# A two-layer decoder trunk in split fp32r matmuls: sums of squares as two fp32r matmuls behind seven k, a gate block copied out of PSUM, input rows 320 floats apart

## The chip, the cores and the metric

One NeuronCore of a Trainium2 chip runs the whole program. The metric is the device time of one execution in microseconds (us); the figure of the kernel before is the median of three runs. One execution was also profiled; its own time and its span (first to last instruction) stand in the table below.

## The reference, cut to what matters

256 tokens of width 1024 go through two layers and a last RMSNorm, all in float32:

```python
hdn = modulate(rmsnorm(x, norm1_g[l]), shift1, scale1)
proj = hdn @ w_in[l]                       # latents, sb q/k/v, mb q/k/v, three gates
q  = rmsnorm(q_lat, q_norm_g[l]) @ w_uq[l]
kv = rmsnorm(c_kv, kv_norm_g[l]) @ w_ukv[l]
merged = g_a * (o_mla @ w_o_mla[l]) + g_b * (o_sb @ w_o_sb[l]) + g_c * (o_mb @ w_o_moba[l])
x = x + gate1[:, None, :] * (merged @ w_out[l])
hdn = modulate(rmsnorm(x, norm2_g[l]), shift2, scale2)
x = x + gate2[:, None, :] * (jnp.square(jax.nn.relu(hdn @ w_ff1[l])) @ w_ff2[l])
```

`rmsnorm` divides a token by the root of its mean square and multiplies by a gain; `modulate` multiplies by 1 + scale and adds a shift. shift, scale and gate come from a conditioning vector (`w_ada`). The gates g_a, g_b, g_c are sigmoids of columns of `proj`.

## The kernel before, in words

**Layout.** Activations lie transposed: the 1024 features are eight tiles (k = 0 to 7) of 128 partitions by 256 tokens. Every float32 product is made of three fp32r matmuls: weights and activations are each split into a high part (rounded to fp32r) and a low part (the rest), and high·high, high·low and low·high are added up in PSUM (`mm3`, L348 to L351, and L983 to L986 for the second MLP product). A sum of squares instead is a plain float32 matmul of a 256-column tile with a matrix of minus ones (`minus`), which adds over the partitions and leaves the sum in every partition (`Rms.sum`, L301).

**Jobs.** The work is a list of jobs. A job is 1 MB of weights fetched by one DMA of the SP queue into one of three buffers, split in four pieces (L184 on ACT for the high part, L185 on DVE for the low part), and used by two or more parts of 24 matmuls each. The parts of a job with `half` (L353) go over k from 0 to 7 inside one half of 128 output features. Splits of later jobs are spread over the parts of earlier ones. Attention and the two latent norms are side tasks, which are let in between parts (`pump`). Outside the stretches named next, a scheduler orders each engine's instructions by program position and readiness, with a cost model of its own; each engine then runs its list strictly in order.

**Buffers.** `mm` is a pool of three PSUM buffers (128 x 2 x 256), which all outputs of such parts take in turn; a new output waits until the reader of the buffer's last content is done. `slot` is a pool of eight large SBUF buffers; `t512` is a pool of four 128 x 2 x 256 ones.

**Seams.** Where a residual update ends and the next normed product begins, an order written by hand takes over (`seam` L869, `overlap` L926, under a manual schedule). There are three such seams: output projection to MLP in layer 0, MLP to the next layer, output projection to MLP in layer 1. A fourth, the tail, makes the last norm. In a seam:
- `ahead` (L815) has already scaled x by its gain without the root, as high and low rows `xh` and `xl` of 258 columns, which are 256 tokens and the shift vector twice. Both are whole slots with rows 258 floats apart, behind a phase of 48 floats.
- `pre_mm` (L366) multiplies these rows with the weights of the next two jobs, a and b (6 matmuls of 258 columns per k and job, 96 in all), since the root can be applied to the product afterwards.
- The sum of squares is made meanwhile: tiles 0 to 5 are added into `acc` on DVE, the squares of tiles 6 and 7 are kept apart (`late`). `sum(more=True)` issues the matmuls of `acc` and of tile 6, then come the last residual update (tile 7) and `pre_mm` of job a for k = 0, 1, 2, then the matmul of tile 7's squares, then k = 3 to 7.
- `root` (L310) is four ACT and three DVE instructions in a chain; two weight pieces of the job after b are split behind it; then `modulate` (L336) makes the finished activation, tile by tile, as a high part on ACT (L342) and a low part on DVE (L345). The job after b is the first that reads this activation, k by k.

**Latent norms.** `lat_norm` (L657) runs twice a layer (2 and 6 tiles) as a side task: squares, adds, `sum`, `root`, then scaled tiles in high and low parts.

**Gates and latent keys.** `gates(1)` makes four blocks of the stick-breaking gate. A block's `done` is `sigmoid` (L133): Abs of the PSUM block on ACT, Exp, Ln, one DVE instruction that reads the PSUM block again (L137), and Exp. Behind the fourth block comes the job of `wukv`: two PSUM blocks `kn` of latent keys, each copied out by four ACT instructions (L741), and two blocks `mvps` of values; then come the jobs of `wuq`.

Of the kernel before, what the change touches and what calls it, by code (L numbers as in the profile page):

```python
# [11 lines left out]
F32 = mybir.dt.float32  # L12
# [9 lines left out]
S = 256  # L22
# [18 lines left out]
def trunk(ctx, tc, xT, heads, pos, signs, masks, gfin, wada, win, wkpe, wuq, wukv, wo, wout, wff1, wff2, out):  # L41
# [7 lines left out]
    def mmps(name):  # L49
        return psum.tile([128, 2, 256], F32, name=name, tag="mm", bufs=3)  # L50
# [7 lines left out]
    def slot(name, dt=F32, shape=(128, 8, 256)):  # L58
        a, b = shape[1:]
        t = big.tile([128, PHASE + 8 * (S + 2)], dt, name=name, tag="slot", bufs=8)  # L60
        return t[:, PHASE:PHASE + a * b].rearrange("p (a b) -> p a b", b=b)

    def t512(name, dt=F32):
        return work.tile([128, 2, 256], dt, name=name, tag="t512", bufs=4)
# [68 lines left out]
    def sigmoid(dst, src, tmp):  # L133
        nc.scalar.activation(tmp, src, AF.Abs)
        nc.scalar.activation(tmp, tmp, AF.Exp, scale=-1.0)
        nc.scalar.activation(tmp, tmp, AF.Ln, bias=1.0)
        nc.vector.scalar_tensor_tensor(tmp, src, 0.0, tmp, op0=OP.min, op1=OP.subtract)  # L137
        nc.scalar.activation(dst, tmp, AF.Exp)
# [101 lines left out]
    def split(dh, dl, src):  # L240
        nc.scalar.activation(dh, src, AF.Copy)
        nc.vector.tensor_sub(dl, src, dh.bitcast(F32))  # L242
# [34 lines left out]
    class Rms:  # L277
# [15 lines left out]
                nc.vector.tensor_add(self.acc, self.acc, sq[:, 0, :])  # L293
            self.i += 1

        def square_late(self, a):
            sq = t256("sql")
            nc.scalar.activation(sq, a, AF.Square)
            self.late.append(sq)

        def sum(self, more=False):  # L301
            if self.ps is None:
                self.ps = mmps("ssum")[:, 0, :]
            terms = ([self.acc] if self.acc is not None else []) + self.late
            for t in terms:
                nc.tensor.matmul(self.ps, minus, t, start=self.first, stop=not more and t is terms[-1])
                self.first = False
            self.acc, self.late = None, []
# [57 lines left out]
    def pre_mm(jb, ps, xg, ks):  # L366
        for k in ks:
            for i in range(2):
                c = k * 256 + i * 128
                for n, (w, a) in enumerate(((jb.wh, xg[0]), (jb.wh, xg[1]), (jb.wl, xg[0]))):  # L370
                    nc.tensor.matmul(ps[:, i, 0:258], w[:, c:c + 128], a[:, k, :], start=k == 0 and n == 0,  # L371
                                     stop=k == KT - 1 and n == 2, skip_group_check=True)

    def job(src, f, kts, act, done, ncol=256, before=None, pre=None):
# [220 lines left out]
    def layer(l):  # L595
# [94 lines left out]
        def gate_done(b, u):  # L690
            def done(ps, j):
                if u == 0:
                    T["g", b] = slot("gate")
                g = T["g", b][:, 2 * u:2 * u + 2, :]
                sigmoid(g, ps, g)
            return done

# [117 lines left out]
        def ahead(k, sec):  # L815
            if sec == 5 and l + 1 == L:
                return
            l2, gofs, sc, sh = (l, 56, 4, 3) if sec == 2 else (l + 1, 48, 1, 0)
            if k == 0:
                rms["gs"] = gs = gain(l2, gofs, sc)  # L820
                rms["xs"] = xh, xl = tuple(slot(n, F32R, (128, KT, S + 2)) for n in ("xh", "xl"))
                m = mods[l2][:, sh * 8:sh * 8 + 8, None].to_broadcast([128, KT, 2])
                split(xh[:, :, S:], xl[:, :, S:], m)
            xh, xl = rms["xs"]
            g = rms["gs"][:, k:k + 1]
            nc.scalar.activation(xh[:, k, :S], x[:, k, :], AF.Copy, scale=g)
            nc.vector.scalar_tensor_tensor(xl[:, k, :S], x[:, k, :], g, xh[:, k, :S].bitcast(F32),
                                           op0=OP.mult, op1=OP.subtract)

        def x_done(u, ps, sec):  # L830
# [9 lines left out]
        def x_last(i, ps, sec):  # L840
            def go():
                x_one(6 + i, ps, sec)
                final(6 + i, sec)
                rms["q"].square_late(x[:, 6 + i, :])
                ahead(6 + i, sec)
            if i == 0:
                go()
            else:
                rms["last"], rms["end"] = go, ps
# [76 lines left out]
        def overlap(then, n):  # L926
            l2, sh = (l, 3) if then == 2 else (l + 1, 0)
            a, b = jobs[n:n + 2]
            split_to(n + 1, PIECES)
            pa, pb = atps("pre0"), atps("pre1")  # L930
            rms["q"].sum(more=True)
            rms["last"]()
            pre_mm(a, pa, rms["xs"], range(3))
            rms["q"].sum()
            pre_mm(a, pa, rms["xs"], range(3, KT))
            split_to(n + 2, PIECES // 2)
            r = rms["q"].root()
            split_to(n + 2, PIECES)
            pre_mm(b, pb, rms["xs"], range(KT))
            modulate(l2, r, rms["gs"], sh, range(KT))  # L940
            skip.update((n, n + 1))
            return lambda: [split_to(later(n, 3), 2), a.pre(pa, r), split_to(later(n, 3), 4), b.pre(pb, r)]
# [332 lines left out]
```

## Time and profile before

| | us |
|---|---|
| Median of three runs | 935.19 (934.09 to 935.22) |
| Profiled execution, its own time | 934.94 |
| Its span | 933.2 |
| PE busy (TensorE matmuls) | 916.7 (98%) |
| DVE busy (VectorE) | 731.0 (78%) |
| ACT busy (ScalarE) | 600.5 (64%) |
| Mean granted TensorE clock | 0.999 of full speed |

PE is the matmul engine, PEld its weight loads, which overlap it. A matmul's record is longer than the distance to the next one's start, because matmuls are pipelined: what a matmul costs in a stream is that distance. A plain float32 matmul leaves two records. In a timeline, neighbouring instructions of one kind are merged ("x2"), and a bracket tells how long the engine sat idle and what ended that. Idle time of an engine other than the bound costs nothing by itself.

### The profile page before, as it was taken

How to read it: one execution, taken by the hardware profiler on the slowest of the kernel's cores; microseconds unless marked ns; L12 is line 12 of the kernel's file. 1: busy time of each engine (PE TensorE's matmuls, PEld its weight loads, DVE VectorE, ACT ScalarE, POOL GpSimd, SP SyncE). 2: the span in 40 equal slices, each digit the busy share in tenths (PEclk: the TensorE clock that was granted, in tenths of full speed). 3: DMA queues.
4: the chain of work that ended last, by engine and by line, in shares of the span. 5: the costliest groups of instructions: out<-in, count | busy, mean ns of one | idle time of the engine just before them, and what ended most of it. 6: DMA issues, size and time to landing. Idle time of an engine off the chain costs nothing.

```text
span 933.2 us, 19188 instructions
## 1 busy us (share of the span) xinstructions
PE 916.7 (98%) x7780; PEld 891.2 (96%) x7781; DVE 731.0 (78%) x1423; ACT 600.5 (64%) x1255; POOL 8.7 (1%) x14
## 2 busy tenths in 40 slices
PE   9999999999999999999999999999999999999997
PEld 6888999899999999999999999989999999999997
DVE  6979789887899986767888877889787989454553
ACT  3577678857676774645566667886667677564642
POOL 0000000000000000000000000000000000000002
PEclk9999999999999999999999999999999999999999
DMA  9956554664767488677947654655666637655531
GB/s 337 401 211 242 168 220 157 221 242 173 256 230 268 143 315 309 228 271 265 341 162 275 226 195 156 218 188 215 236 210 242 219 143 282 255 181 192 179 132 46
DMA packets 34074, 208.77 MB, mean 224 GB/s; under 512 B 3905, under 2 KB 4802, under 8 KB 11458
## 3 DMA queue, kind: packets, MB, share of 16 engines
q1 hardware_dynamic: 33696, 207.09, 62.0%
q8 instruction: 61, 1.00, 0.4%
q10 hardware_dynamic: 146, 0.26, 0.1%
q0 software_dynamic: 144, 0.20, 0.1%
q14 instruction: 27, 0.22, 0.1%
HBM read 206.49 MB, written 1.05 MB: 222 GB/s over the span
## 4 chain that ended last, share of the span: by engine, by line
PE 81%; DVE 9%; DMA 5%; ACT 4%; issue 1%; SPq 0%; DVEq 0%; ACTq 0%
PE ps L349 15%; PE ps L350 15%; PE ps L351 15%; PE ff L984 5%; PE ff L983 5%; PE ff L986 5%; PE pre L371 4%; DVE wl L185 3%; DMA ws<-win 3%; DMA adaw<-wada 2%; ACT wh L184 1%; PE po L476 1%; PE vps L349 1%; PE vps L350 1%; PE vps L351 1%; PE s L531 1%
## 5 line engine op out<-in xcount | busy, mean ns | idle before, releaser
L185 DVE TENSOR_TENSOR wl<-ws,wh 128x512 fp32r<-128x512 f32 (+1 forms) x592 | 378.8, 673 | 132.2 <-ACT wh L184 131.7
L184 ACT ACTIVATE wh<-ws 128x512 fp32r<-128x512 f32 (+1 forms) x592 | 337.3, 615 | 206.1 <-PE ps L350 108.3
L349 PE MATMUL ps<-act,wh 128*128 128x256 f32 x1120 | 312.4, 279 | 0.0
L351 PE MATMUL ps<-act,wl 128*128 128x256 f32 x1120 | 310.6, 277 | 0.0
L350 PE MATMUL ps<-act,wh 128*128 128x256 f32 x1120 | 310.5, 277 | 0.0
L350 PEld LDWEIGHTS ps<-act,wh 128*128 128x128 f32 x1120 | 211.0, 188 | 0.1
L349 PEld LDWEIGHTS ps<-act,wh 128*128 128x128 f32 x1120 | 210.5, 188 | 0.5 <-DVE wl L185 0.2
L351 PEld LDWEIGHTS ps<-act,wl 128*128 128x128 f32 x1120 | 210.4, 188 | 0.0
L983 PE MATMUL ff<-fh,wh 128*128 128x256 f32 x448 | 123.6, 276 | 0.0
L984 PE MATMUL ff<-fl,wh 128*128 128x256 f32 x448 | 123.6, 276 | 0.0
L986 PE MATMUL ff<-fh,wl 128*128 128x256 f32 x448 | 123.6, 276 | 0.0
L249 DVE SCALAR_TENSOR_TENSOR ws<-ws,cb 128x1024 f32<-128x1024 f32 x80 | 95.8, 1219 | 16.1 <-DMA ws<-wada 15.8
L986 PEld LDWEIGHTS ff<-fh,wl 128*128 128x128 f32 x448 | 84.1, 188 | 0.0
L983 PEld LDWEIGHTS ff<-fh,wh 128*128 128x128 f32 x448 | 84.1, 188 | 0.0
L984 PEld LDWEIGHTS ff<-fl,wh 128*128 128x128 f32 x448 | 84.1, 188 | 0.0
L551 ACT ACTIVATE e<-s,st 128x128 f32<-128x128 f32 (+1 forms) x64 | 25.9, 431 | 23.9 <-DVE st L546 18.7
L371 PE MATMUL pre<-xh,wh 128*128 128x258 f32 x96 | 28.3, 295 | 0.0
L350 PE MATMUL ps<-ml,wh 128*128 128x256 f32 x96 | 26.8, 281 | 0.5 <-DVE ml L242 0.5
L371 PE MATMUL pre<-xh,wl 128*128 128x258 f32 x96 | 27.1, 283 | 0.0
L371 PE MATMUL pre<-xl,wh 128*128 128x258 f32 x96 | 27.1, 282 | 0.0
L349 PE MATMUL vps<-wh,act 128*128 128x256 f32 x96 | 26.9, 280 | 0.0
L350 PE MATMUL vps<-wl,act 128*128 128x256 f32 x96 | 26.7, 278 | 0.0
(283 smaller groups left out, 1740.3 us busy)
## 6 DMA issues: line engine op xcount, KB each, us to landing
ws<-wff SPq DMA_DIRECT2D x64, 1024.0 KB, 4.9
ws<-win SPq DMA_DIRECT2D x50, 1024.0 KB, 4.9
ws<-wada SPq DMA_DIRECT2D x40, 1024.0 KB, 4.9
ws<-wo SPq DMA_DIRECT2D x12, 1024.0 KB, 4.9
adaw<-wada SPq DMA_DIRECT2D x16, 512.0 KB, 7.3
ws<-wout SPq DMA_DIRECT2D x8, 1024.0 KB, 4.9
ws<-win SPq DMA_DIRECT2D x24, 256.0 KB, 7.8
ws<-wuq SPq DMA_DIRECT2D x6, 768.0 KB, 4.3
```

Source lines behind the costliest of these rows:

```text
L184: nc.scalar.activation(job.wh[:, a], job.ws[:, a], AF.Copy)
L185: nc.vector.tensor_sub(job.wl[:, a], job.ws[:, a], job.wh[:, a].bitcast(F32))
L249: nc.vector.scalar_tensor_tensor(w, w, 1.0, cb, op0=OP.mult, op1=OP.mult, accum_out=mods[l][:, 2 * b + i:2 * b + i + 1])
L349: nc.tensor.matmul(o, wh, ah, start=first, stop=False)
L350: nc.tensor.matmul(o, wh, al, start=False, stop=False)
L351: nc.tensor.matmul(o, wl, ah, start=False, stop=last)
L371: nc.tensor.matmul(ps[:, i, 0:258], w[:, c:c + 128], a[:, k, :], start=k == 0 and n == 0, stop=k == KT - 1 and n == 2, skip_group_check=True)
L476: nc.tensor.matmul(po[64 * h:64 * h + 64, u, o:256], v[:, k, vc:vc + 64], pT[:, h, c:c + n], start=k == 0, stop=k == 1, tile_position=(0, ...
L551: nc.scalar.activation(e[:, h, a:b], s[:, h, a:b], AF.Exp, scale=scale, bias=st[:, 4 + c:5 + c], accum_out=st[:, 8 + c:9 + c])
L983: nc.tensor.matmul(o, wh[:, c0:c0 + 128], fh[:, k, :], start=st, stop=False, skip_group_check=True)
L984: nc.tensor.matmul(o, wh[:, c0:c0 + 128], fl[:, k, :], start=False, stop=False, skip_group_check=True)
L986: nc.tensor.matmul(o, wl[:, c0:c0 + 128], fh[:, k, :], start=False, stop=en, skip_group_check=True)
```

## The change

The diff, cut to its core:

```diff
-        def square_late(self, a):
+        def square_late(self, a, add=False):
             sq = t256("sql")
             nc.scalar.activation(sq, a, AF.Square)
-            self.late.append(sq)
+            if add:
+                nc.vector.tensor_add(self.acc, self.acc, sq)
+            else:
+                self.late.append(sq)
 
         def sum(self, more=False):
             if self.ps is None:
                 self.ps = mmps("ssum")[:, 0, :]
+            if not self.late and not more:
+                t = t512("sqr", F32R)
+                split(t[:, 0, :], t[:, 1, :], self.acc)
+                for i in range(2):
+                    nc.tensor.matmul(self.ps, neg_ones, t[:, i, :], start=i == 0, stop=i == 1)
+                self.acc = None
+                return
...
-                    nc.tensor.matmul(ps[:, i, 0:258], w[:, c:c + 128], a[:, k, :], start=k == 0 and n == 0,
+                    nc.tensor.matmul(ps[:, i, 0:258], w[:, c:c + 128], a[k][:, :S + 2], start=k == 0 and n == 0,
...
+                if b == 1 and u == 3:
+                    raw = t512("graw")
+                    nc.scalar.activation(raw, ps, AF.Copy)
+                    ps = raw
                 sigmoid(g, ps, g)
...
-                rms["xs"] = xh, xl = tuple(slot(n, F32R, (128, KT, S + 2)) for n in ("xh", "xl"))
-                m = mods[l2][:, sh * 8:sh * 8 + 8, None].to_broadcast([128, KT, 2])
-                split(xh[:, :, S:], xl[:, :, S:], m)
-            xh, xl = rms["xs"]
+                rows = [slot(n, F32R, (128, 6, 320)) for n in ("x0", "x1", "x2")]
+                rms["xs"] = [[rows[j // 6][:, j % 6, :] for j in range(i, i + KT)] for i in (0, KT)]
...
-                rms["q"].square_late(x[:, 6 + i, :])
+                rms["q"].square_late(x[:, 6 + i, :], True)
...
             pa, pb = atps("pre0"), atps("pre1")
-            rms["q"].sum(more=True)
             rms["last"]()
-            pre_mm(a, pa, rms["xs"], range(3))
+            pre_mm(a, pa, rms["xs"], range(KT - 1))
             rms["q"].sum()
-            pre_mm(a, pa, rms["xs"], range(3, KT))
+            pre_mm(a, pa, rms["xs"], range(KT - 1, KT))
```

In a seam all eight squares are now added into `acc` on DVE, `acc` is split into a high and a low part, and two fp32r matmuls with the minus ones add them up, once seven of the eight k of job a have been issued. The two latent norms of a layer sum in the same way, at their old places. The tail keeps its own matmuls, but tile 6 is added into `acc` there too. The sixteen rows of a seam lie 320 floats apart in three slots of six rows; the shift columns are written by two ACT and three DVE instructions in place of one each. The fourth block of the stick-breaking gate is copied to SBUF by ACT first, and `sigmoid` reads the copy.

## Rows read from the trace of the kernel before

**Rows 1.** The page's first part: busy time of the engines
```profile
PE 916.7 (98%) x7780; PEld 891.2 (96%) x7781; DVE 731.0 (78%) x1423; ACT 600.5 (64%) x1255; POOL 8.7 (1%) x14
```

**Rows 2.** Timeline of PE around the first seam (start us, us, what)
```profile
293.33 0.28 PE L351 MATMUL xl<-mh,wl 128*128 128x256 f32 x1
...
298.21 0.59 PE L306 MATMUL ssum<-sacc,negs 128*128 128x256 f32 x2
...
301.26 0.60 PE L306 MATMUL ssum<-sql,negs 128*128 128x256 f32 x2
...
311.04 0.28 PE L349 MATMUL ps<-act,wh 128*128 128x256 f32 x1
...
313.56 0.28 PE L350 MATMUL ps<-act,wh 128*128 128x256 f32 x1
```

**Rows 3.** The chain that ended last, in order of time: pieces of two seams
```profile
298.37 0.86 PE ssum L306 x4
...
301.86 9.35 PE pre L371 x78
474.43 0.86 PE ssum L306 x4
```

**Rows 4.** Timeline of ACT in the first seam
```profile
301.89 0.47 ACT L312 ACTIVATE y<-ssum,eps 128x256 f32<-128x256 f32 x1 [0.87 <-PE ssum L306]
```

**Rows 5.** Timeline of DVE in the first seam
```profile
298.65 0.47 DVE L806 SCALAR_TENSOR_TENSOR x<-xl,mod,x 128x256 f32<-128x256 f32 x1
...
304.18 1.29 DVE L185 TENSOR_TENSOR wl<-ws,wh 128x512 fp32r<-128x512 f32 x2
...
306.44 0.49 DVE L345 SCALAR_TENSOR_TENSOR act<-ht,mod,act 128x256 fp32r<-128x256 f32 x1 [0.18 <-ACT act L342]
...
311.86 0.48 DVE L345 SCALAR_TENSOR_TENSOR act<-ht,mod,act 128x256 fp32r<-128x256 f32 x1 [0.18 <-ACT act L342]
```

**Rows 6.** Timeline of PE around the second latent norm's sum, layer 0
```profile
153.10 0.59 PE L306 MATMUL ssum<-sacc,negs 128*128 128x256 f32 x2
...
153.65 0.28 PE L350 MATMUL ps<-act,wh 128*128 128x256 f32 x1
...
159.77 0.28 PE L351 MATMUL ps<-act,wl 128*128 128x256 f32 x1
...
161.89 0.28 PE L351 MATMUL ps<-act,wl 128*128 128x256 f32 x1
```

**Rows 7.** Who waited for whom (us in total, times, longest)
```profile
PE mvps L349 <- DVE gate L137: 3.0, 2, 1.5
```

**Rows 8.** Timeline of PE behind the latent keys, layer 0
```profile
164.84 1.25 PE L567 MATMUL pt<-head,e 128*128 128x128 f32 x10
167.60 0.47 PE L349 MATMUL mvps<-wh,lath 128*128 128x512 f32 x1 [1.50 <-DVE gate L137]
...
170.57 0.36 PE L349 MATMUL ps<-lath,wh 128*128 128x256 f32 x1
```

**Rows 9.** Timeline of ACT in the same stretch
```profile
163.13 0.58 ACT L134 ACTIVATE gate<-ps 128x512 f32<-128x512 f32 x1
...
165.68 1.94 ACT L741 ACTIVATE km<-kn 64x256 f32<-64x256 f32 x5
...
168.16 1.17 ACT L741 ACTIVATE km<-kn 64x256 f32<-64x256 f32 x3
```

**Rows 10.** Timeline of PE in the output projection of layer 1
```profile
728.54 0.38 PE L349 MATMUL ps<-mh,wh 128*128 128x256 f32 x1 [0.16 <-ACT mh L241]
...
729.78 0.37 PE L350 MATMUL ps<-ml,wh 128*128 128x256 f32 x1
729.99 0.28 PE L351 MATMUL ps<-mh,wl 128*128 128x256 f32 x1
...
730.82 0.28 PE L349 MATMUL ps<-mh,wh 128*128 128x256 f32 x1
```

**Rows 11.** Timeline of PE's weight loads in the tail
```profile
924.91 0.52 PEld L897 LDWEIGHTS tsum<-negs,sql 128*128 128x128 f32 x4 [0.20 <-ACT sql L298]
```

More of the change, by code (lines that the diff above doesn't have):

```diff
@@ L820, in ahead @@
                 rms["gs"] = gs = gain(l2, gofs, sc)
-                rms["xs"] = xh, xl = tuple(slot(n, F32R, (128, KT, S + 2)) for n in ("xh", "xl"))
-                m = mods[l2][:, sh * 8:sh * 8 + 8, None].to_broadcast([128, KT, 2])
-                split(xh[:, :, S:], xl[:, :, S:], m)
-            xh, xl = rms["xs"]
+                rows = [slot(n, F32R, (128, 6, 320)) for n in ("x0", "x1", "x2")]
+                rms["xs"] = [[rows[j // 6][:, j % 6, :] for j in range(i, i + KT)] for i in (0, KT)]
+                for t, p, k0, n in ((0, 0, 0, 6), (1, 0, 6, 2)):
+                    m = mods[l2][:, sh * 8 + k0:sh * 8 + k0 + n, None].to_broadcast([128, n, 2])
+                    nc.scalar.activation(rows[t][:, p:p + n, S:S + 2], m, AF.Copy)
+                for k0, n, t, p in ((0, 4, 1, 2), (4, 2, 2, 0), (6, 2, 2, 2)):
+                    m = mods[l2][:, sh * 8 + k0:sh * 8 + k0 + n, None].to_broadcast([128, n, 2])
+                    h = rows[0][:, k0:k0 + n, S:S + 2] if k0 < 6 else rows[1][:, 0:2, S:S + 2]
+                    nc.vector.tensor_sub(rows[t][:, p:p + n, S:S + 2], m, h.bitcast(F32))
+            xh, xl = (a[k] for a in rms["xs"])
             g = rms["gs"][:, k:k + 1]
-            nc.scalar.activation(xh[:, k, :S], x[:, k, :], AF.Copy, scale=g)
-            nc.vector.scalar_tensor_tensor(xl[:, k, :S], x[:, k, :], g, xh[:, k, :S].bitcast(F32),
+            nc.scalar.activation(xh[:, :S], x[:, k, :], AF.Copy, scale=g)
+            nc.vector.scalar_tensor_tensor(xl[:, :S], x[:, k, :], g, xh[:, :S].bitcast(F32),
                                            op0=OP.mult, op1=OP.subtract)
```

## The prediction

> **What bounds the kernel now.** I read the page's first part (which engine is full), then the list of waits and the chain that ended last (where the full engine still stands, and for whom), then the timelines of PE, ACT and DVE around each place that the diff touches (how much each would have to spare). PE is busy for 916.7 of 933.2 us [rows 1]: nearly every matmul slot counts, and PE's idle time lies in a few places. So a saved matmul is worth its distance to the next start, as long as what PE reads next is ready; where it is not, the chain on ACT and DVE sets the time.
>
> Three prices recur. A 256-column fp32r matmul in a stream takes 113.5 ns: 43 of them start between 293.33 and 298.21 [rows 2]. The same stream also has a slower pace: 18 matmuls between 159.77 and 161.89 take 117.8 ns each, and that stretch begins behind a plain float32 sum at 153.10 [rows 6]. One plain float32 sum costs 0.43 (four records in 0.86 [rows 3]). A 258-column matmul of a seam takes 119.9 ns (78 in 9.35 [rows 3]).
>
> **The change, part by part.**
>
> *PE work in a seam.* Three float32 sums (1.29) go, two fp32r matmuls (0.23) come: 1.06 less. The 96 matmuls of `pre_mm` took 119.9 ns behind a float32 sum, where the pace was slow in rows 6 as well. Without such a sum ahead, and with aligned rows, I take the fast pace, 113.5 x 258/256 = 114.4 ns; the bounds are 119.9 and 114.4. Gain on PE: 96 x 5.5 ns = 0.53. If nothing waited, a seam would be 1.6 shorter.
>
> The Trainium skill (TensorE: Matmul & The Clock Gate, "Back-to-back issue gap") states a warm gap of N/2.4 + 2.5 ns, which is 109.2 for 256 columns and 110.0 for 258. The rows show 113.5 and 119.9, so this kernel does not reach it; by the page's figure the seven k below would end 0.18 earlier, and each seam with them (+0.19 for the first instead of +0.37).
>
> *What the seam waits for.* Set the first seam's times by its first matmul behind the output projection, at 298.21 [rows 2]. Before, the last sum starts at 301.26 and `root` at 301.89 [rows 2, 4]. The first part of the next activation's low half starts at 306.44, the last at 311.86 and ends 312.34 [rows 5]. PE first reads this activation at 311.04, and the low part of k = 7 (the 23rd matmul) at 313.56 [rows 2]. So PE has 1.2 us to spare: that is the slack that the move spends.
>
> After, 42 matmuls of 114.4 ns (4.80) stand ahead of the sum. It starts at 303.01, its second matmul at 303.12; with the record's 0.28 and the 0.03 that `root` took to follow, `root` starts at 303.43, 1.54 later than now. Its inputs are there: from the last residual update (298.65, ended 299.12 [rows 5]) the chain has a square, an add, a high copy and a low part, at most 0.49 each by the 256-column rows there, so about 301.1. One new wait is on DVE: the add waits for ACT's square of tile 7, and behind it queue the low row of tile 7, the low part of the sum and two weight splits; all of them end before 303. That is the cover, and without it (a sum that is 2 us late) the two matmuls would hold PE.
>
> From `root` on nothing is shorter. It is a chain, then two weight splits that stand on DVE ahead of `modulate` (304.18 [rows 5]), then low parts 0.77 apart on DVE, whereas PE takes one k each 0.34. So the last low part ends at 312.34 + 1.54 = 313.88. PE would want it 1.6 earlier than now, at 311.95. It waits in short pieces from about k = 3 on, 1.9 in all, and passes k = 7 at 313.93: **0.37 later than before**, not 1.6 earlier. What is late next is the activation, not the sum. The other bound: with 119.9 ns the sum is 0.23 later, so +0.60; with a pace of 113.5 it is hardly earlier, +0.33. The third seam is entered at the slow pace (rows 10: 0.118 apart from 729.99 to 730.82), so I take 118.7 ns there: +0.55. **Three seams: +1.3 us** (+0.9 to +1.8).
>
> *Latent norms.* Four float32 sums (0.43) become two fp32r matmuls (0.23): 0.2 less each, and a copy on ACT and a subtraction on DVE more. Two of them (the first of each layer) count in full: **−0.4**. The two at 153.10 and its twin lie ahead of a PE wait, so what they gain is lost there. The nearest price for PE waiting on the new split is one ACT and one DVE instruction, 0.9; above nothing is lost if the scheduler puts the sum later in PE's list.
>
> *Gate block.* Twice PE waits for the fourth gate block's second reading on DVE, 1.50 each [rows 7, 8]. With the copy that PSUM block comes free at about 163.7, when its first ACT reading ends now [rows 9]. PE is at its end of transposes at 166.1 (164.84 + 1.25 [rows 8]), so this wait goes. But the copy is one more ACT instruction (0.58), ahead of the eight copies of the latent keys, which run from 165.68 to 169.33 with one other instruction between [rows 9]. The three PSUM blocks go round: the second value block needs the first key block, the first `wuq` block needs the second one. So `wuq` starts when the eighth copy ends, 169.33 + 0.5 = 169.85, instead of 170.57 [rows 8]: 0.7 less per layer, **−1.4**. Bounds: 0.3, if the split of the norm's sum also lands ahead of the copies; 2.1, if the copies run early enough that only PE's own work counts (1.5, 0.2 of the sum, and 95 matmuls at the fast pace, 0.4).
>
> *The rest.* Three slots instead of two: two live tiles and three new ones are under eight, nothing waits. The three extra small shift instructions run during the projection, where DVE and ACT have room (78% and 64% [rows 1]). In the tail one float32 sum goes, but PE still waits there for tile 7's squares [rows 11]: nothing. No DMA is added, moved or passed, on SP or POOL.
>
> **Sum:** +1.3 − 0.4 − 1.4 = −0.5. Against the profiled execution's own 934.94 (span 933.2 and 1.7 around it) that is 934.4; the median stands 0.25 above this execution, so **934.7**. Its own range is 933.0 to 936.5.
>
> **The rivals.**
>
> *A, the seam's gain arrives whole.* It needs `modulate` to end 1.9 earlier than I reckon. For it: PE saves 1.6 in each seam. Against: the split and DVE order in rows 5 have no idle gap to squeeze. 3 x −1.6 − 1.8 = −6.6: 928.6.
>
> *B, the gate region gives all.* The copies of the keys move ahead. For it: the scheduler orders ACT anew. Against: ACT has no pause there [rows 9]. 2 x −2.1 − 0.4 + 1.3 = −3.3, and up to 0.4 a layer more if the fast pace lasts behind it: 931.1 to 931.9.
>
> *C, slower: the waits leave PE at the slow pace.* Place: the last wait of a seam. Behind the wait at 728.54, which the row shows as idle time, the 11 starts to 729.78 came 113 ns apart; behind the one at 729.78, so short that the row shows no idle time (only a longer record), the seven from 729.99 to 730.82 came 118 apart [rows 10]. From 311.04 to the next seam at 474.43 [rows 2, 3] lie about 1,440 matmuls; 4.5 ns each is 6.5. One such stretch gives 941, both (the third seam has another) 948. It decides if the final wait is of the short kind; by the distances above mine are some 0.3 to 0.4 each, long enough to show as idle time, like the harmless one.
>
> *D, the split sums hold PE in the four norms* for about 0.8 each: 937.9.
>
> *E, the row pitch does nothing.* The slow pace of rows 6 came with rows 256 floats apart, so a float32 sum ahead, not the pitch, may be what slows `pre_mm`; and if both stay as they are, 119.9 ns is kept: +0.23 a seam, 935.2 to 935.4, inside the forecast, since the activation sets the seam anyway. The Trainium skill (SBUF — State Buffer, "Door 1: The DMA port swizzle (why `[64,N]` ≈ `[32,N]`)") says that consecutive accesses run at full bandwidth in 16-byte lines; rows of either pitch are read consecutively, so by it 320 floats gain nothing.
>
> **How the numbers follow.** A measurement of this kernel can tell about 0.2% (1.9 us), so faster means below 933.3 and slower above 937.1. Forecast with E 0.57, A 0.08, B 0.16, C 0.10, D 0.09. Faster: A, B and 0.07 of the forecast's lower edge, 0.31. Slower: C and most of D, 0.18. Within: 0.51. The range leaves out A and C: 930.6 to 938.2.
>
> **What would show it.** In a seam after: `root` starts some 5.2 behind the first 258-column matmul, PE shows about 1.9 of waits for DVE L345 in the first half behind `pre_mm`, each under 0.5; the 258-column distance falls to 114 to 115. PE no longer waits for the gate's DVE instruction but for copies of the latent keys. Sums show 0.11 apart. I am wrong if the job behind the seam starts without waits (A), if the MLP stream runs at 118 ns (C), or if PE stands before a sum (D).

## The result, and the profile after

The changed kernel takes 945.41 us (median of four runs, 942.87 to 953.2) against 935.21 for the kernel before in the same runs: a ratio of 1.0119, 95% interval 1.0082 to 1.0156. It is 1.2% slower. The forecast was 934.7, and its range ended at 938.2. The profiled execution took 947.07 us, its span is 945.3. Ratios leave out executions more than 1.5% above the fastest of their version (944.49 us in one version below, 943.92 and 946.66 in another), while medians and ranges keep them.

The page's first part. PE is still what bounds the kernel, with 7.2 us more of busy time and 16 instructions fewer than in [rows 1]:

```profile
PE 923.9 (98%) x7764; PEld 896.1 (95%) x7765; DVE 737.5 (78%) x1443; ACT 605.0 (64%) x1267; POOL 8.7 (1%) x14
```

From the list of waits, the lines in which PE or its weight loads (PEld) wait inside the stretches that the diff touches, and one other (`po`). The wait of [rows 7] is gone, two others stand in its place:

```profile
PEld mvps L359 <- ACT km L755: 4.3, 2, 2.2
PEld ps L360 <- DVE act L355: 4.1, 12, 0.4
PE mvps L359 <- ACT km L755: 3.9, 2, 1.9
...
PE po L486 <- DVE mbqk L596: 2.4, 1, 2.4
...
PE ps L360 <- DVE act L355: 1.5, 9, 0.2
```

**Where the 12.1 us between the two spans came from.** The n-th matmul into each output was matched in both traces; the difference of their starts grows as follows (us, places by the clock of before):

| stretch | grows by | what stands there |
|---|---|---|
| start to 95 | +3.5 | one wait of 2.4 (the `po` line above) with half the clock behind it; only +1.1 in the next trace of this kernel |
| 95 to 162 | −1.0 | latent sums, and the faster pace behind them |
| 162 to 171 | +2.0 | latent keys, layer 0 |
| 171 to 298 | −0.9 | stretches at the other pace |
| 298 to 320 | +1.0 | first seam |
| 320 to 470 | +5.9 | MLP of layer 0, no wait in it |
| 470 to 490 | +1.0 | second seam |
| 490 to 612 | −1.0 | as 95 to 162 |
| 612 to 620 | +2.1 | latent keys, layer 1 |
| 620 to 747 | −1.1 | stretches at the other pace |
| 747 to 770 | +0.8 | third seam |

**The MLP.** The view of two stretches of 100 us, first after, then before (PE, PEld, DVE, ACT and POOL as busy us and instructions; granted clock; DMA share; GB/s):

```profile
340.00:440.00 100.00, 100.00 (x852) 100.00 (x851) 67.65 (x117) 53.26 (x102) 0.00 (x0) 1.00 0.71 254
780.00:880.00 100.00, 100.00 (x884) 100.00 (x884) 61.89 (x100) 60.84 (x114) 0.00 (x0) 1.00 0.64 231
```

```profile
340.00:440.00 100.00, 100.00 (x885) 100.00 (x884) 69.97 (x119) 56.33 (x106) 0.00 (x0) 1.00 0.75 273
780.00:880.00 100.00, 100.00 (x885) 100.00 (x884) 58.06 (x92) 57.09 (x107) 0.00 (x0) 1.00 0.61 215
```

PE is 100% busy in all four lines and the granted clock is 1.00 in all four, yet the first 100 us hold 852 matmuls instead of 885: 117.8 against 113.3 ns from start to start (a count takes in two or three that began ahead of the window). The busy share can't show this; the count in a window does. From 318.07 to the next seam start 1,417 matmuls at that pace: 1,417 x 4.5 ns = 6.4 us. In the second MLP the changed kernel has the fast pace.

**The first seam**, timelines of PE, ACT and DVE:

```profile
301.84 0.40 PE L381 MATMUL pre<-x,wh 128*128 128x258 f32 x2
...
306.90 0.40 PE L311 MATMUL ssum<-sqr,negs 128*128 128x256 f32 x2
...
313.62 0.28 PE L359 MATMUL ps<-act,wh 128*128 128x256 f32 x1
...
316.39 0.39 PE L360 MATMUL ps<-act,wh 128*128 128x256 f32 x1 [0.17 <-DVE act L355]
...
317.85 0.38 PE L360 MATMUL ps<-act,wh 128*128 128x256 f32 x1
318.07 0.28 PE L361 MATMUL ps<-act,wl 128*128 128x256 f32 x1
```

```profile
307.34 0.47 ACT L322 ACTIVATE y<-ssum,eps 128x256 f32<-128x256 f32 x1 [1.70 <-PE ssum L311]
```

```profile
317.31 0.49 DVE L355 SCALAR_TENSOR_TENSOR act<-ht,mod,act 128x256 fp32r<-128x256 f32 x1 [0.18 <-ACT act L352]
```

Times here are counted, as in the prediction, from the first matmul behind the output projection: after, that is the first 258-column one at 301.84, before, the first float32 sum at 298.21 [rows 2]. The sum stands 5.06 behind it and `root` 5.50 (3.68 before, by [rows 2, 4]). The job behind the seam starts 11.78 behind it, 1.05 earlier than before ([rows 2]: 12.83). Then it waits in pieces, 1.8 us by the time that its 24 matmuls take (4.45 for 23 distances, against 23 x 0.1133), and the low part of k = 7 is read at 317.85, 0.66 later than before. From 318.07 on the pace is 117.8 ns. In the third seam the last wait has the same size, and the pace behind it is 113.3:

```profile
775.04 0.38 PE L360 MATMUL ps<-act,wh 128*128 128x256 f32 x1
775.27 0.28 PE L361 MATMUL ps<-act,wl 128*128 128x256 f32 x1
```

**The latent keys**, timelines of PE and ACT, and the windows of 2 us:

```profile
168.63 0.60 PE L577 MATMUL pt<-head,e 128*128 128x128 f32 x4
171.16 0.60 PE L359 MATMUL mvps<-wh,lath 128*128 128x512 f32 x1 [1.93 <-ACT km L755]
171.56 0.63 PE L360 MATMUL mvps<-wl,lath 128*128 128x512 f32 x1
...
173.69 1.60 PE L577 MATMUL pt<-head,e 128*128 128x128 f32 x8
175.04 0.37 PE L359 MATMUL ps<-lath,wh 128*128 128x256 f32 x1
```

```profile
166.50 0.58 ACT L707 ACTIVATE graw<-ps 128x512 f32<-128x512 f32 x1
...
169.57 2.73 ACT L755 ACTIVATE km<-kn 64x256 f32<-64x256 f32 x7
```

```profile
169.00:171.00 2.00, 0.23 (x3) 0.00 (x0) 2.00 (x5) 1.97 (x6) 0.00 (x0) 1.00 0.83 323
171.00:173.00 2.00, 1.84 (x5) 1.46 (x6) 1.79 (x4) 1.94 (x6) 0.00 (x0) 0.60 0.06 17
173.00:175.00 2.00, 2.00 (x10) 1.71 (x9) 0.56 (x1) 1.98 (x5) 0.00 (x0) 0.54 0.65 176
```

Before, ten transposes stood ahead of the value blocks [rows 8] and two behind them. Now four stand between the two blocks and eight behind: the scheduler has given the filler away, and PE stands 1.93 us for the copies of the keys. These start at 169.57, 1.4 later than before relative to the key block ([rows 9]: 165.68; PE is 2.5 later at this point). In the windows behind the wait the granted clock is 0.54 to 0.60, so for most of them at the lower of its two levels (1.2 and 2.4 GHz): the two 512-column matmuls shown start 0.40 apart, where those of the block ahead of the transposes start 0.23 apart.

### The profile page after: what moved, and what is told of

Its sections match the earlier page's. It is cut to its first block, busy times and chain, and to the rows that moved or that the text cites. A ratio compares the mean times of both kernels' runs of the same rounds, so it can differ in the third digit from the quotient of the medians.

```text
span 945.3 us, 19187 instructions
## 1 busy us (share of the span) xinstructions
PE 923.9 (98%) x7764; PEld 896.1 (95%) x7765; DVE 737.5 (78%) x1443; ACT 605.0 (64%) x1267; POOL 8.7 (1%) x14
## 3 DMA queue, kind: packets, MB, share of 16 engines
HBM read 206.49 MB, written 1.05 MB: 220 GB/s over the span
## 4 chain that ended last, share of the span: by engine, by line
PE 80%; DVE 7%; DMA 6%; ACT 6%; issue 1%; SPq 0%; DVEq 0%; ACTq 0%
PE ps L359 15%; PE ps L360 15%; PE ps L361 15%; PE ff L1002 5%; PE ff L1005 5%; PE ff L1003 5%; DMA ws<-win 3%; DVE wl L185 2%; DMA adaw<-wada 2%; PE pre L381 2%; PE po L486 2%; ACT wh L184 1%; DMA ws<-wada 1%; PE vps L359 1%; PE vps L360 1%; PE vps L361 1%
## 5 line engine op out<-in xcount | busy, mean ns | idle before, releaser
L381 PE MATMUL pre<-x,wh 128*128 128x258 f32 x192 | 35.0, 284 | 0.0
L381 PEld LDWEIGHTS pre<-x,wh 128*128 128x128 f32 x192 | 29.8, 191 | 0.0
L381 PE MATMUL pre<-x,wl 128*128 128x258 f32 x96 | 27.2, 283 | 0.0
L359 PE MATMUL ps<-mh,wh 128*128 128x256 f32 x96 | 26.7, 280 | 0.1
```

The costliest lines, as they stand in the source:

```text
L359: nc.tensor.matmul(o, wh, ah, start=first, stop=False)
L381: nc.tensor.matmul(ps[:, i, 0:258], w[:, c:c + 128], a[k][:, :S + 2], start=k == 0 and n == 0, stop=k == KT - 1 and n == 2, skip_group_che ...
```

## The experiments

### The changed kernel again

No edit.

> The changed kernel once more, nothing edited. Theory (the waits that the seams now have leave PE at one of two paces, and which one varies from execution to execution): the times fall into steps of about 6.4 us above some 942 (942, 948, 955 for none, one and two slow stretches), and in this profile the stretch behind the first seam need not be the slow one. Rival (the change fixes the slow pace behind seam 1): again 117.8 ns per 256-column matmul from about 318 to 485 us and 113.3 ns behind the two other seams, every time at 946 to 948.

946.06 (942.54 to 947.27, six runs). The trace shows the same picture: 117.8 ns behind the first seam (852 starts in 340 to 440), 113.3 behind the others. The steps of 6.4 us are not seen between these six runs, only to the 953.2 of the first four. So both traces of this kernel have the slower pace behind the first seam, and by their times most of its other executions do too; the rival holds in that, without its cause being told.

### The chain of the seam made shorter

```diff
-            split_to(n + 2, PIECES // 2)
+            split_to(n + 2, PIECES)
             r = rms["q"].root()
-            split_to(n + 2, PIECES)
             pre_mm(b, pb, rms["xs"], range(KT))
```

> The changed kernel with all four pieces of the next weight split ahead of root instead of two ahead and two behind. Theory (the last activation is what the seam waits for, and its waits decide the pace): modulate starts 1.2 us earlier, the waits of PE for the activation's low part (4.1 us in 12 places with one job's matmuls in the changed kernel) all but go, each seam is 1.0 to 1.3 us shorter, no stretch runs at 117.8 ns: 938 to 941 with a spread under 1.5 us. Rival (the slow pace comes from elsewhere, from the fp32r sums or the row pitch): 942 to 949 with the same spread as the changed kernel.

941.61, but from 933.51 to 946.2: five runs of twelve at 933.5 to 934.8, seven at 941.0 to 946.2. The waits of PE's weight loads for the activation fall from 4.1 us in 12 places to 1.7 in 6, and the seams cost −0.1, −0.1 and 0.0 against before, 0.8 to 1.1 less than in the changed kernel: this half of the theory holds. The other, that no stretch would run at 117.8 ns, is missed: with short waits left, the first and the last stretch behind a seam still did so in the trace (946.2). By its five low executions, this version without such stretches would be 1 us faster than the kernel before; what costs the most is the pace.

### The gate block alone, and left out

The copy alone in the kernel before, and the changed kernel without it:

```diff
+                if b == 1 and u == 3:
+                    raw = t512("graw")
+                    nc.scalar.activation(raw, ps, AF.Copy)
+                    ps = raw
                 sigmoid(g, ps, g)
```

> The kernel before with the copy of the fourth gate block alone. Theory (with the copy the scheduler orders PE anew: of the ten transposes that stood ahead of the value blocks four stand between them and the rest behind, so PE has nothing to do while ACT copies the keys): PE waits some 2 us per layer for the copies of the keys, the clock falls there, the wuq job starts 1.0 to 2.1 later, 936.5 to 939.5 us. Rival (the prediction): the wuq job starts 0.7 earlier, 933.8 us.

> The changed kernel without the copy of the gate block. Theory: the wait behind the keys goes back to the one of before (1.5 us for the gate's DVE instruction), 1 to 2 us per layer less than the changed kernel up to the first seam, 940 to 942 us in executions without a slow stretch, 946 to 948 with one. Rival (the copy gains 0.7 a layer as predicted): 1.4 us more than the changed kernel, 944 to 946 without a slow stretch.

Alone: 935.64, ratio 0.9998 (0.9989 to 1.0008). PE has the new order here too, but waits half as long, and the clock stays at 1.00, so the theory's 936.5 to 939.5 is missed:

```profile
166.03 0.60 PE L567 MATMUL pt<-head,e 128*128 128x128 f32 x4
167.55 0.50 PE L349 MATMUL mvps<-wh,lath 128*128 128x512 f32 x1 [0.91 <-ACT km L745]
...
169.83 0.37 PE L349 MATMUL ps<-lath,wh 128*128 128x256 f32 x1
```

`wuq` starts 0.5 earlier in either layer, counted from the first matmul of the keys, near the 0.7 of the prediction; at the end nothing of it is left. Some 17 us behind the start of `wuq` PE waits 0.9 and 1.3 for `qm`, the queries that DVE copies (0.2 in one place before), and stretches behind that come out at the other pace:

```profile
PE s L528 <- DVE qm L782: 2.1, 2, 1.3
```

Without the copy the changed kernel takes 936.37: eight runs of twelve at 933.9 to 936.5, four at 941.5 to 947.3. My price of 1 to 2 us a layer explains the step at the keys, not all that came off: by their times, more of the executions without the copy had the fast pace in both MLPs, though no line of a seam was edited. The one traced (941.79) still has the slower pace behind the first seam.

### The other parts alone

Rows 320 floats apart in three slots, alone; and the latent sums alone:

```diff
-            q.sum()
+            t = t512("sqr", F32R)
+            split(t[:, 0, :], t[:, 1, :], q.acc)
+            q.ps = mmps("ssum")[:, 0, :]
+            for i in range(2):
+                nc.tensor.matmul(q.ps, neg_ones, t[:, i, :], start=i == 0, stop=i == 1)
             r = q.root()
```

> The kernel before with the input rows 320 floats apart in three slots, nothing else. Theory (the pitch does nothing): pre_mm stays at 119.9 ns a matmul and the time within 1 us of the kernel before, 934 to 936. Rival (the step of my prediction: aligned rows bring the fast pace): 114.4 ns, each seam 0.5 shorter on PE.

One run, 941.29, but the rows are not its cause. The chain of what ended last shows a seam's second part as

```profile
302.69 9.43 PE pre L371 x78
```

which is 120.9 ns a matmul, against 119.9 in [rows 3]: the pitch brings nothing. Its three seams cost +0.1, +0.5 and +0.1. The loss of this run stands elsewhere: PE waits 1.82 us at 639.42 for a DVE copy, and the granted clock is 0.50 from 640 to 646, which together cost 4.8.

> The kernel before with the sums of the two latent norms as two fp32r matmuls each, nothing else. Theory (read from the changed kernel without the gate copy, where the wuq job gains 0.8 us in each layer): the stream behind the second norm runs at 113.3 instead of 117.8 ns and the wuq job starts 0.8 earlier in each layer; what is left at the end is 933 to 935, as stretches behind it may take the other pace. Rival (the prediction): 0.2 a layer, 934.8.

933.17, ratio 0.9974 (0.9964 to 0.9985): faster than the kernel before. From 154 to 164 the windows (before, then this version) hold 91 matmuls instead of 87, at a granted clock of 1.00 in both, and `wuq` starts 0.8 earlier in either layer, as the theory had it and four times the prediction's 0.2:

```profile
154.00:164.00 10.00, 10.00 (x87) 10.00 (x86) 8.95 (x29) 9.94 (x31) 0.00 (x0) 1.00 0.30 106
154.00:164.00 10.00, 10.00 (x91) 10.00 (x90) 9.51 (x29) 9.94 (x29) 0.00 (x0) 1.00 0.30 106
```

So behind this norm the float32 sum leaves the slower pace and the fp32r sum the faster one. The same holds in each trace here, in both layers: 117.8 ns in 10 of 10 cases with float32 matmuls in this place (five kernels), 113.3 in 30 of 30 with fp32r ones (fifteen traces).

Both together, the gate copy and the latent sums, with the seams of before:

> The kernel before with the gate copy and the fp32r sums of the latent norms, seams as before. Alone the latent sums gave 933.2 us and the gate copy no change. Theory (the two spoil each other: the sums bring PE to the value blocks earlier, the copy takes the transposes from ahead of them, so PE stands 1.9 us for the copies of the keys instead of 0.9, and behind so long a wait the granted clock falls to half in some executions): a wait of 1.9 us for the copies of the keys in each layer, 932 to 933 where the clock holds, 1.6 to 2.7 us more for each layer in which it falls: a median of 934 to 937, above the latent sums alone. Rival (the two gains add up): 931.5 to 932.5.

934.71 (933.6 to 938.01), ratio 0.9989 (0.9977 to 1.0002). The gains don't add up, as no run reaches the rival's 931.5 to 932.5; whether it is slower than the latent sums alone is not clear, as the intervals of the two ratios overlap. Both layers have the same wait of 1.93, at 168.24 and 617.18; the windows show the clock hold behind the first and fall behind the second:

```profile
168.00:170.00 2.00, 1.76 (x9) 1.44 (x10) 1.87 (x4) 1.94 (x6) 0.00 (x0) 1.00 0.08 24
170.00:172.00 2.00, 2.00 (x20) 2.00 (x18) 0.56 (x1) 1.98 (x5) 0.00 (x0) 1.00 0.64 135
617.00:619.00 2.00, 1.82 (x8) 1.50 (x9) 1.81 (x4) 1.94 (x6) 0.00 (x0) 0.91 0.02 6
619.00:621.00 2.00, 2.00 (x11) 2.00 (x10) 0.56 (x1) 1.98 (x5) 0.00 (x0) 0.50 0.69 168
```

Up to the `wuq` job the keys cost 0.4 where it holds and 1.4 where it falls.

### Waits without any fp32r sum in the seam

```diff
-            pre_mm(a, pa, rms["xs"], range(3))
+            pre_mm(a, pa, rms["xs"], range(6))
             rms["q"].sum()
-            pre_mm(a, pa, rms["xs"], range(3, KT))
+            pre_mm(a, pa, rms["xs"], range(6, KT))
```

and the same with 7.

> The kernel before with the last float32 sum of a seam behind six k instead of three: no fp32r sum, no other row pitch, no copy of the gate. Theory (a wait on the activation makes the pace a matter of chance): root 2.2 us later, PE waits some 1.0 us for the activation in each seam, 938 without a slow stretch, and in a part of the executions 6 or 12 us more, so that the spread is over 5 us. Rival (the slow stretches come from the fp32r sum or the pitch): 938 to 939 with the narrow spread of the kernel before, all stretches behind seams at 113.3 ns.

939.04 (937.6 to 939.92). The wait is 1.1 a seam, as expected, but both MLP stretches are fast (only the short stretch behind the second seam is not) and the spread is narrow: nearly the rival's numbers.

> The kernel before with its last float32 sum behind seven k. Behind six k the waits left every stretch behind a seam at 113.3 ns. Theory (the pace that a wait leaves depends on when the last wait ends against PE's own steps, and is nearly fixed for one order of instructions): root 0.72 later, 0.6 to 0.7 more waiting per seam, 941; and with the waits at other places the stretches behind the seams may come out at 117.8 ns, 947 or 953, in most executions or in none. Rival (only kernels with fp32r sums in the seam get slow stretches): 940.5 to 941.5 and 113.3 ns.

944.47 (941.08 to 950.53, five runs). The profiled one, 950.53, has the slower pace in the second MLP, behind float32 sums and rows 258 floats apart:

```profile
340.00:440.00 100.00, 100.00 (x884) 100.00 (x884) 71.34 (x122) 56.63 (x107) 0.00 (x0) 1.00 0.74 271
780.00:880.00 100.00, 100.00 (x852) 100.00 (x851) 59.51 (x97) 57.24 (x108) 0.00 (x0) 1.00 0.63 222
```

So neither the fp32r sum nor the pitch is needed for it. A wait behind the seam is enough to open the pace; how it falls differs between six k and seven, with one trace of each.

### The sum behind five k

```diff
-            pre_mm(a, pa, rms["xs"], range(KT - 1))
+            pre_mm(a, pa, rms["xs"], range(5))
             rms["q"].sum()
-            pre_mm(a, pa, rms["xs"], range(KT - 1, KT))
+            pre_mm(a, pa, rms["xs"], range(5, KT))
```

> The changed kernel with the sum behind five k of job a instead of seven, nothing else edited. The split of the sum is ready 3.2 us behind the first 258-column matmul in the changed kernel's first seam, and 30 matmuls of 120 ns are 3.6 us, so PE doesn't wait for it. Theory (the late activation makes the waits, and the waits make the pace a matter of chance): root comes 1.4 us earlier, the job behind waits 0.5 us or less instead of 1.9, each seam is 0.9 to 1.2 shorter than in the changed kernel; where a short wait is left the pace behind it is still either 113.3 or 117.8 ns, so the times lie near 938 or 6 us above; with no wait left they lie within 1.5 us. Rival (the two fp32r sums or the longer row pitch slow the stream): 942 to 948 as the changed kernel.

934.47 (931.81 to 939.34), ratio 0.9983 (0.9965 to 1.0001). Each seam is 0.7 shorter than in the kernel before, so 1.5 to 1.7 shorter than in the changed one: more than expected. This alone takes back what the change lost.

> The changed kernel with the sum behind five k and without the gate copy. Theory (with both faults out, what is left is gain: the seams 0.67 each, as traced with five k; the latent sums 0.8 a layer): 935.3 - 2.0 - 1.6 = 931.7 us, 930.5 to 933.5. Rival (the short wait that is left in a seam still makes slow stretches): a part of the executions near 938.

> The same with the input rows 258 floats apart in two slots, as in the kernel before. Theory (the pitch does nothing): the same time as with rows of 320 floats within 1 us, pre_mm at 120 ns a matmul. Rival: over 1 us slower.

937.45 (928.23 to 944.49) and 937.73 (932.84 to 941.26). The theory's 931.7 is missed: the lowest runs are there (928.2, 930.7, 930.8), most are not. The pitch makes no difference again. The rival was right, and the faults that I had named were not all of them.

### No wait at all behind the seam

Both edits together, the sum behind five k and the four pieces ahead of `root`; the second run without the gate copy.

> The changed kernel with the sum behind five k and all four weight pieces ahead of root, gate copy kept. With five k alone a wait of 0.33 us was left in each seam; the pieces moved ahead take some 0.7 off the chain on DVE. Theory (only where PE waits for the activation is the pace behind a seam open): PE waits nowhere in the job behind a seam, each seam is 1.0 shorter than in the kernel before, the stretch behind it runs at one pace in every execution, and if that is the fast one, as in the kernels before without such a wait, the times lie at 932 to 935 with a spread under 4 us, which the gate region makes. Rival (fp32r sums and pitch make the pace change): again executions at 938 to 945.

> The same without the gate copy: seams without a wait and the latent sums. Theory: 935.4 - 3.0 - 1.6 = 930.8, 929.5 to 932.5, spread under 3 us: faster than both kernels. Rival as in the run above: a part of the executions 6 us higher.

933.66 (932.17 to 944.56; ten of twelve up to 936.2, two at 944.5) and 939.5 (929.41 to 946.66). In the first a wait is left in each seam, too short to show as idle time of PE; its trace is of one of the two slow executions and has the fast pace behind the first seam and the slower one behind the others. In the second the job behind the first seam starts without a wait, and the stretch is slower from its first matmul on (timeline of PE, then the window):

```profile
310.51 0.40 PE L381 MATMUL pre<-x,wh 128*128 128x258 f32 x2
310.76 0.28 PE L381 MATMUL pre<-x,wl 128*128 128x258 f32 x1
310.88 0.28 PE L359 MATMUL ps<-act,wh 128*128 128x256 f32 x1
310.99 0.28 PE L360 MATMUL ps<-act,wh 128*128 128x256 f32 x1
311.11 0.28 PE L361 MATMUL ps<-act,wl 128*128 128x256 f32 x1
```

```profile
340.00:440.00 100.00, 100.00 (x852) 100.00 (x851) 67.33 (x118) 54.72 (x104) 0.00 (x0) 1.00 0.72 259
```

The theory that only a wait opens the pace falls here. What each kernel whose three seams were all fast in its trace had, and this one lacks, is a plain float32 matmul in the seam.

### A float32 matmul put back

In the kernel just shown (gate copy out, four pieces ahead of `root`):

```diff
-            pre_mm(a, pa, rms["xs"], range(5))
-            rms["q"].sum()
-            pre_mm(a, pa, rms["xs"], range(5, KT))
+            pre_mm(a, pa, rms["xs"], range(3))
+            q = rms["q"]
+            q.ps = mmps("ssum")[:, 0, :]
+            nc.tensor.matmul(q.ps, minus, x[:, 0, :], start=True, stop=True)
+            pre_mm(a, pa, rms["xs"], range(3, 4))
+            q.sum()
+            pre_mm(a, pa, rms["xs"], range(4, KT))
```

> The changed kernel without the gate copy, all four weight pieces ahead of root, one plain float32 matmul more behind three k (its result is overwritten) and the fp32r sum behind four k. PE should wait nowhere behind a seam, as without that matmul. Theory (a plain float32 matmul in the seam with no wait behind it brings the stream to the fast pace; of the seams traced so far 18 of 18 of that kind ran at 113.3, of the others about half): all stretches behind seams at 113.3 ns, lowest times of the kernel without it (929.4, 930.6) plus 3 x 0.43: 930.7 to 932.5, spread under 4 us. Rival (fp32r sums or pitch make the pace change, whatever else stands there): again a part of the executions 6 and 12 us higher, up to 947.

931.51 (930.55 to 932.44, five runs), ratio 0.9951 (0.9938 to 0.9964). With a matmul whose result nobody reads the kernel is some 8 us faster in the median, and the spread closes from over 12 us to 2. The edit also moves the fp32r sum from behind five k to behind four, and no run has the one without the other:

```profile
340.00:440.00 100.00, 100.00 (x885) 100.00 (x884) 71.18 (x125) 54.97 (x104) 0.00 (x0) 1.00 0.75 276
780.00:880.00 100.00, 100.00 (x885) 100.00 (x884) 57.76 (x92) 57.84 (x110) 0.00 (x0) 1.00 0.62 215
```

The same matmul behind three k, with the sum left behind seven and the split pieces where the change has them (the waits stay):

> The changed kernel without the gate copy, with the same extra float32 matmul behind three k but the fp32r sum where the change has it, behind seven k, so that the waits for the activation stay. Theory (a wait behind the seam opens the pace again, float32 matmul or not, as behind the float32 sums at seven k): 935.5 to 938 where all is fast and executions 6 us or more above that. Rival (the float32 matmul alone decides): 935.5 to 938, none above 940.

940.49 (935.89 to 945.7, seven of twelve above 940). The profiled one, 935.89, is fast behind all three seams and has the same 4.1 us of PEld's waits as the changed kernel; the others weren't traced. The same version without the float32 matmul (the gate copy left out, above) took 936.37, with a ratio of 1.0021 (0.9995 to 1.0047) against 1.0052 (1.0033 to 1.0071) here. So where the waits stay, the float32 matmul brings nothing that the times show.

Counted over the traces, seams behind which the stretch ran at 117.8 ns (from the second 24 matmuls on): none of 24 with a plain float32 matmul and no wait behind (eight kernels); 3 of 9 with both (three kernels); 13 of 27 without a float32 matmul (nine traces, three of those seams without any wait, 2 of them slow).

### Better than both

The latent sums, and in a seam float32 sums as before, but fewer. Two (tile 6 added into `acc`, tile 7 kept apart):

> The kernel before with the fp32r latent sums, and in a seam tile 6's squares added into the running sum on DVE, so that two float32 sums are left instead of three; everything else as before. Theory (a float32 sum that goes is worth its 0.43 as long as no wait comes in its place): 933.2 - 1.3 = 931.9, spread as the latent sums alone, no wait behind a seam. Rival (the add of tile 6 comes too late on DVE and PE waits ahead of the seam's first sum): 933 to 934.

931.52 (929.9 to 932.65), ratio 0.9953 (0.9935 to 0.9971), 0.4 better than expected. One sum of all eight squares behind four k:

```diff
-                rms["q"].square_late(x[:, 6 + i, :])
+                rms["q"].square_late(x[:, 6 + i, :], True)
...
-            rms["q"].sum(more=True)
             rms["last"]()
-            pre_mm(a, pa, rms["xs"], range(3))
+            pre_mm(a, pa, rms["xs"], range(4))
             rms["q"].sum()
-            pre_mm(a, pa, rms["xs"], range(3, KT))
+            pre_mm(a, pa, rms["xs"], range(4, KT))
```

> The kernel before with the fp32r latent sums, and in a seam all eight squares added on DVE and one plain float32 sum behind four k, rows and gate as before. Theory (two float32 sums of 0.43 go from each seam, the chain is not later: the sum starts 2.9 us behind the first 258-column matmul instead of 3.05 and nothing is split for it): 933.2 - 3 x 0.86 = 930.6, no wait behind a seam, 113.3 ns, spread under 4 us; the best kernel so far. Rival (the adds on DVE make root late, a wait comes in place of the sums): 932 or more, with slow stretches in a part of the executions.

931.4 (929.8 to 933.75), ratio 0.9955 (0.9942 to 0.9968). No wait behind a seam and 113.3 ns behind all three, but not better than two sums: the first and third seam gain 0.9 and 0.8, the second nothing, as PE waits 0.8 there for the add. With the kernel of the float32 matmul put back these are three versions some 0.45% faster than before.

## Why the prediction was wrong, point by point

**What bounds the kernel:** right. PE has 98% in either kernel, and each loss is one of PE's.

**Pace of `pre_mm`:** the step "Without such a sum ahead, and with aligned rows, I take the fast pace", 114.4 ns, failed. 42 matmuls take 5.06, so 120.5 ns. Rival E was right: the pitch does nothing, and no float32 sum slows these 258-column streams. The rule cited there (the Trainium skill, SBUF — State Buffer, "Door 1: The DMA port swizzle (why `[64,N]` ≈ `[32,N]`)"), by which 320 floats gain nothing, agrees with the 120.9 ns of the pitch alone.

**The activation as what is late:** right in kind and nearly in size. `root` came 5.50 behind the first matmul (5.2 predicted), the waits sum to 1.8 (1.9), and k = 7 is read 0.66 later; the bound with 119.9 ns was 0.60, the value taken 0.37. Three seams cost 2.8 by the table (0.66 of the first one's 1.0 stands up to k = 7), against 1.3 forecast and 1.8 at the bound.

**Latent norms:** too small. The two sums were worth 0.8 a layer, not 0.2: behind them the stream keeps the fast pace, which I had left as a bound inside the gate's term. The step that failed is "what they gain is lost there", at the wait behind: with the latent sums alone that wait grows from 1.50 to 1.80, so most of the gain passes.

**Gate block:** −0.7 a layer alone was near (−0.5 measured up to `wuq`), but it was the wrong sum. The step by which PE is "at its end of transposes at 166.1" and "this wait goes" took PE's order as fixed, and the copies of the keys as starting at 165.68. The scheduler moved the transposes behind the value blocks, PE came there earlier by the latent sums, and ACT copied later. In the changed kernel the term is +2.0 and +2.1 instead of −1.4 for both; that PE would wait for the copies of the keys was forecast, not for how long. The part of the clock is 1.6 a layer: with the same 1.93 wait the version with all pieces ahead of `root` held the clock and gained 0.6, the changed kernel lost 1.0 a layer (from 95 and from 490 to the start of `wuq`), as did the one with five k in layer 0.

**The pace behind a seam:** this decided the result. The sum put the pace of the MLP stretches at no change; behind the first seam it cost 5.9, half of the 12.1. Rival C named the place, the price (6.5 a stretch; the table has 5.9 up to 470) and the time (941 for one stretch), but got a chance of 0.10 on a rule read from one pair of rows: that a wait of the short kind, without idle time in its row, leaves the slower pace, and a longer one doesn't. The last wait in the first seam is of that short kind (317.85), so the forecast failed by its own rule; but in the third seam of the changed kernel a last wait of the same size (775.04, a record of 0.38 as at 317.85) left the fast pace. The rule read from [rows 10] doesn't hold. What should have been read from the trace of before is that all three of its seams leave the fast pace, though the stream ahead of the third runs at the slower one [rows 10], and that the change takes away the one thing in the seam which differs from the streams around it. That trace also has the contrary case: behind the second latent norm a float32 sum leaves the slower pace [rows 6]. That in a seam the float32 matmul brings the fast pace, if no wait follows, is borne out by 24 seams and by putting one back, though that edit moved the sum too; it is no rule for other places, and why it does so is not known.

**What stays open:** why the same kernel takes the slower pace behind its first seam in all traces and the fast one behind its third; why without the gate copy, by the times, it was fast more often, while with the sum behind five k leaving the copy out raised the median (934.47 to 937.45, and 933.66 to 939.5 with all pieces ahead of `root`; the intervals of the ratios overlap); what makes a float32 matmul go with the fast pace in a seam and with the slower one behind a latent norm; and when a wait of 1.9 us brings the clock down.

## What to carry to other kernels

Count the starts in a window of a stream that is 100% busy: two paces 4% apart can hide in it, and a stretch of 1,400 matmuls makes 6 us of that. Before taking an odd instruction out of a regular stream for its own time (here 0.43 us), look at what pace the stream has ahead of it and behind it, and measure more than a few executions, since a change can turn a fixed pace into a matter of chance. A copy that frees a buffer earlier also tells a scheduler to order anew: price the new order, and with it the filler that the old one had put into the wait.

## What the runs showed of the hardware

**Two paces of one stream.** A stream of weight loads and 256-column fp32r matmuls runs at 113.3 or 117.8 ns a matmul at a granted clock of 1.00, and keeps the one it has for over 1,400 matmuls. The Trainium skill (TensorE: Matmul & The Clock Gate, "Back-to-back issue gap") says that the spacing in such a stream is set by the weight loads and the matmuls together, through a window in which they may be reordered; two spacings would not contradict that, but no run here shows the mechanism. The N/2.4 + 2.5 ns that the prediction took from that section is given there for an isolated matmul; it makes 109.2 for 256 columns, and neither pace here reaches it.

**In a seam, a plain float32 matmul went with the fast one**, in 24 of 24 seams with no wait behind it, also where the stream ahead ran at 117.8 ns. Behind the second latent norm it was the other way about: 117.8 ns in 10 of 10 cases with float32 sums, 113.3 in 30 of 30 with fp32r ones. So the kind of matmul alone does not set the pace.

**The clock falls behind short waits.** Behind waits of 1.93 and 1.82 us the granted clock went to half for some 3 to 7 us, and behind others of 1.93 and 1.81 it stayed at 1.00. So a wait of this length can cost more than twice itself: 1.82 us of waiting came with a loss of 4.8 in all.
